# Routing by pairs of heads, dot products that write to PSUM, and a row ring over dead activations, in a one-core decoder block

## The chip, the cores and the metric

The kernel runs on one core of a Trainium2 chip. The metric is device time in microseconds (us) of one launch; lower is better. Engines are named as in the profile: PE (TensorE matmul), PEld (its weight load), DVE (VectorE), ACT (ScalarE), POOL (GpSimd), SP (SyncE, which here only issues DMAs).

## What is computed

One decoder block over 256 tokens of 2048 features, all in float32. The first half (projection, sliding-window attention, retention, gates, output projection) is not touched. The second half is a product-key expert layer:

```python
qry = (xt @ w_query).reshape(T, H, 2, 128)                 # H = 8 heads
s = jnp.einsum('thpd,phnd->thpn', qry, sub_keys)           # 2 x 128 scores a head
top_s, top_i = lax.top_k(s, 16)
cand_s = top_s[:, :, 0, :, None] + top_s[:, :, 1, None, :]
best_s, best_pos = lax.top_k(cand_s.reshape(T, H, 256), 16)
expert_idx = ...                                           # 128 experts a token, of 16384
gates = jax.nn.softmax(best_s, axis=-1)
act = gelu(einsum('td,thkd->thk', xt, expert_down[expert_idx]))
y = einsum('thk,thkd->td', gates * act, expert_up[expert_idx])
out = rmsnorm(h + y, final_norm)
```

## The kernel before, in words

Tokens lie on the 128 partitions in two blocks (`NB = 2`). A matrix product in float32 is done as three passes over operands that are split in a high and a low part: ACT casts a weight unit to `whi` (L107), DVE subtracts to get `wlo` (L108), PE does three matmuls (L138 to L140, L154 to L156). A unit is 4 x 128 rows of 512 columns (1 MB), loaded by SP into a ring of three `raw` tiles; `whi` and `wlo` are rings of three half units. Units are requested two ahead.

The expert layer's stages follow one another:

- **Queries.** Four products of 4 units (`gemm(h_ops, 4)`). After each, `query_scores` makes the scores `sc` for 4 lists of 128 keys (two heads) in each token block.
- **Routing** (DVE): `top16` finds the 16 best of a list with five instructions; `candidates`, `cand_top`, `ranks` and `pick` follow for all 8 heads of a token block; `indices` writes `ix`, the row numbers.
- **gemm1.** The dot products with all 16384 experts over features 0 to 1407, in 32 tiles of 512 experts. A tile is two split units (48 matmuls of 512 columns) and a third unit of 3 x 128 features that PE takes directly as float32 (L161; operand `htf`, the sum of `hth` and `htl`). The result goes to `a_dram`.
- **Dots.** The remaining 640 features: for each of the 256 (block, choice) pairs POOL gathers one expert row of 640 floats per token by an indirect DMA (`fetch_u`, L605), and DVE multiplies it with `hg` and sums (`dot`, L613). The elementwise product goes to `djunk`, which nobody reads.
- **Tail.** For each of the 256 pairs POOL gathers the score from `a_dram` (`score`, L640; 14 ahead) and the 2048-wide row of `expert_up` (`fetch`, L583), in one fixed line; DVE adds weight times row to `ys` in PSUM (L689).

What DVE has to do besides the split is queued by `later(cost, ...)`, and `drain(budget)` takes from that queue after every unit. This settles the order in which code is emitted; a list scheduler with a simulated timeline then sets the order on each engine, and units that are prefetched have priority. Each engine runs its instructions strictly in that order. Rows of both kinds share one ring of `VR = 8` tiles of 2048 floats in the pool `v`, which takes the place of the routing's tiles once routing is over.

Of the kernel before, what the change touches and what calls it, by code (L numbers as in the profile page):

```python
# [16 lines left out]
OP = mybir.AluOpType  # L17
# [12 lines left out]
BG_NATIVE = 4.9  # L30
CF = 8
CN = 3
CG = NC - CF - CN
GC = CG * P
G0 = D - GC
DOT = 0.85
VR = 8
GRP = 8
LEAD = 14


@with_exitstack
def hybrid_block(ctx, tc, x, x_t, anorm, fnorm, frow, w_in, w_ab, w_rb, w_out, w_q, skeys, down, down_n, down_g, up, sinks, fin,
# [26 lines left out]
    for t in range(NT):  # L70
        units += [down[t, u] for u in range(CF // 4)] + [down_n[t]]
# [16 lines left out]
    def emit_unit(u):  # L88
        if units[u].shape[1] == CN:
            nat = stream.tile([P, 4, 512], F32, name="raw", bufs=3)  # L90
            nc.sync.dma_start(nat[:, :CN], units[u])
            ready[u] = nat
            return
        raw = stream.tile([P, 4, 512], F32, name="raw", bufs=3)
        if u == 0:
            for i in range(4):
                nc.sync.dma_start(raw[:, i], units[u][:, i])
        else:
            nc.sync.dma_start(raw, units[u])
        hs = []  # L100
        for i in range(2):
# [3 lines left out]
            for k in range(0, 2, step):  # L105
                src = raw[:, 2 * i + k:2 * i + k + step]
# [37 lines left out]
    def gemm_mixed(ops, xf):  # L144
        ps = [acc.tile([P, 512], F32, name="acc") for _ in range(NB)]
        for u in range(CF // 4):
            hs = next_unit()
            for k in range(4):
                hi, lo = hs[k // 2]
                wh, wl = hi[:, k % 2], lo[:, k % 2]  # L150
                c = u * 4 + k
                for b in range(NB):
                    xh, xl = ops(c, b)
                    nc.tensor.matmul(ps[b], lhsT=xh, rhs=wh, start=(c == 0), stop=False)  # L154
                    nc.tensor.matmul(ps[b], lhsT=xh, rhs=wl, start=False, stop=False)  # L155
                    nc.tensor.matmul(ps[b], lhsT=xl, rhs=wh, start=False, stop=False)  # L156
            drain(BG_RATE)
        nat = next_unit()
        for k in range(CN):
            for b in range(NB):  # L160
                nc.tensor.matmul(ps[b], lhsT=xf[:, k, b * P:(b + 1) * P], rhs=nat[:, k], start=False,  # L161
                                 stop=(k == CN - 1))
        drain(BG_NATIVE)
# [24 lines left out]
    xth = keep.tile([P, NC, T], F32R, name="xth", tag="xh")  # L188
    xtl = keep.tile([P, NC, T], F32R, name="xtl", tag="xl")
# [249 lines left out]
    hth = keep.tile([P, NC, T], F32R, name="hth", tag="xh")  # L439
    htl = keep.tile([P, NC, T], F32R, name="htl", tag="xl")  # L440
# [16 lines left out]
    htf = peer.tile([P, CN, T], F32, name="htf")  # L457
    nc.vector.tensor_add(htf, hth[:, CF:CF + CN].bitcast(F32), htl[:, CF:CF + CN].bitcast(F32))
# [15 lines left out]
    top = rp.tile([P, NB, NC, 16], F32, name="top")  # L474
    topi = rp.tile([P, NB, NC, 16], U32, name="topi")
# [16 lines left out]

    def query_scores(b, j, ps):
# [10 lines left out]
        sc = rp.tile([P, 4, P], F32, name="sc", bufs=6)  # L504
        nc.scalar.copy(sc, pt)
        for i in range(4):
            later(1.0, top16, top[:, b, 4 * j + i], topi[:, b, 4 * j + i], sc[:, i])

    for j in range(4):
        ps = gemm(h_ops, 4)  # L510
        for b in range(NB):
            query_scores(b, j, ps[b])

    rb = [dict() for _ in range(NB)]

    def candidates(b):
        tif = rp.tile([P, NC, 16], BF16, name="tif")
        nc.vector.tensor_copy(tif, topi[:, b])
        cand = rp.tile([P, 8, 136], F32, name="cand")
        tv = top[:, b].rearrange("p (h s) k -> p h s k", s=2)  # L520
        nc.vector.tensor_add(cand[:, :, :128].rearrange("p h (a c) -> p h a c", c=16),
                             tv[:, :, 0, :8, None].to_broadcast([P, 8, 8, 16]),
                             tv[:, :, 1, None, :].to_broadcast([P, 8, 8, 16]))
        nc.vector.tensor_add(cand[:, :, 128:], tv[:, :, 0, 8:], tv[:, :, 1, 0:1].to_broadcast([P, 8, 8]))
        best = rp.tile([P, 8, 16], F32, name="best")
        pos = rp.tile([P, 8, 16], U32, name="pos")
        rb[b].update(tif=tif, cand=cand, best=best, pos=pos)

    def cand_top(b, hd):
        d = rb[b]  # L530
        top16(d["best"][:, hd], d["pos"][:, hd], d["cand"][:, hd])

    def ranks(b):
        d = rb[b]
        bits = rp.tile([P, 2, 8, 16], U32, name="bits")
        nc.vector.tensor_single_scalar(bits[:, 0], d["pos"], 4, op=OP.logical_shift_right)
        nc.vector.tensor_single_scalar(bits[:, 1], d["pos"], 15, op=OP.bitwise_and)
        rf = rp.tile([P, 2, 8, 16], F32, name="rf")
# [7 lines left out]
        ga = rp.tile([P, 8, 16], F32, name="ga")  # L546
        best = d["best"]
        nc.vector.tensor_sub(ga, best, best[:, :, 0:1].to_broadcast([P, 8, 16]))
        nc.scalar.activation(ga, ga, AF.Exp)
        gs = rp.tile([P, 2, 8], F32, name="gs")  # L550
        nc.vector.tensor_reduce(gs[:, 0], ga, axis=AX.X, op=OP.add)
        nc.vector.reciprocal(gs[:, 1], gs[:, 0])
        nc.vector.tensor_mul(sel[:, 2, b].rearrange("p (h k) -> p h k", h=8), ga,
                             gs[:, 1, :, None].to_broadcast([P, 8, 16]))

    def pick(b, s):
        d = rb[b]
# [8 lines left out]
        nc.vector.tensor_add(sel[:, s, b].rearrange("p (h k) -> p h k", h=8), oh[:, :, 0], oh[:, :, 1])  # L566

    for b in range(NB):
        later(2.0, candidates, b)
        for hd in range(8):  # L570
            later(1.0, cand_top, b, hd)
        later(2.0, ranks, b)
        later(4.6, pick, b, 0)
        later(4.6, pick, b, 1)
    ix = peer.tile([P, 2, NB, P], U32, name="ix")
    vtiles = {}
    vp = {}

    def fetch(n):
        v = vp["pool"].tile([P, D], F32, name="v", bufs=VR)  # L580
# [5 lines left out]
    def indices():  # L586
        rt.close()
        msk.close()
        tmp2 = pool("tmp2")
        ef = tmp2.tile([P, 2, NB, P], F32, name="ef")  # L590
        nc.vector.scalar_tensor_tensor(ef[:, 0], sel[:, 0], 128.0, sel[:, 1], op0=OP.mult, op1=OP.add)
        for b in range(NB):
            nc.vector.tensor_scalar_add(ef[:, 1, b], ef[:, 0, b], rows[:, b:b + 1])
        nc.vector.tensor_copy(ix, ef)
        vp["pool"] = pool("v")
        vp["ps"] = pool("ysum", space=PSUM)
        for n in range(VR):
            fetch_u(n)
# [160 lines left out]
```

## Time and profile before

| | |
|---|---|
| median of 3 runs | 2119.17 us (2112.92 to 2120.25) |
| the profiled execution: time, span | 2116.2 us, 2114.4 us |
| PE, DVE, POOL busy | 1387.9, 1556.2, 918.4 us |
| first query matmul | 776.9 us |
| gemm1, first and last matmul | 873.1, 1411.7 us |
| dots, first and last | 971.5, 1397.0 us |
| first score gather, last `expert_up` gather | 1422.2, 2086.7 us |

Times inside the span count from its start. A share of the whole span says little here, since each stage has another limit; the stages are read apart.

### The profile page before, as it was taken

The page shows a single profiled execution, that of the slowest core. Times are in us where ns is not written, and L with a number is a line of the kernel's source. Part 1 is how long each engine was busy: PE and PEld are TensorE (multiplying, and loading weights), DVE is VectorE, ACT ScalarE, POOL GpSimd, SP SyncE. Part 2 cuts the span into 40 slices and gives each one's busy share as a digit, 9 for nine tenths or more (in the row PEclk, how much of TensorE's full clock was granted, in tenths as well). Part 3 has the DMA queues.
Part 4 walks back from the last instruction along what each step waited for, and adds up shares of the span by engine and source line. Part 5 has one row for each costly group of instructions (what it writes and reads, how often), then busy time and mean ns, then how long its engine had stood idle before and what let it go on. Part 6 is the DMA issues. An engine that isn't in the chain of part 4 may idle for free.

```text
span 2114.4 us, 18649 instructions
## 1 busy us (share of the span) xinstructions
PE 1387.9 (66%) x5864; PEld 1076.1 (51%) x5864; DVE 1556.2 (74%) x2037; ACT 614.7 (29%) x780; POOL 918.4 (43%) x802
## 2 busy tenths in 40 slices
PE   8999999999999999999999999960000000000000
PEld 6888888888888888866666676640000000000000
DVE  5676576544544567796777877748989899999998
ACT  6555444444444454433333333310000001000001
POOL 0101001000000000006888888857777777777773
PEclk9999999999999999999999999985555555555555
DMA  8545545655555564559999999987999999999997
GB/s 313 183 151 176 175 144 197 221 197 187 193 189 192 191 231 162 176 194 325 406 406 391 391 408 408 396 353 271 395 397 395 399 399 384 410 400 407 399 400 307
DMA packets 114516, 630.24 MB, mean 298 GB/s; under 512 B 21872, under 2 KB 22512, under 8 KB 54000
## 3 DMA queue, kind: packets, MB, share of 16 engines
q0 software_dynamic: 65536, 352.50, 42.3%
q1 hardware_dynamic: 38016, 253.77, 33.0%
q10 hardware_dynamic: 10864, 22.77, 2.8%
q8 instruction: 46, 0.75, 0.1%
q14 instruction: 54, 0.44, 0.1%
HBM read 610.10 MB, written 18.87 MB: 297 GB/s over the span
## 4 chain that ended last, share of the span: by engine, by line
PE 47%; DMA 20%; issue 17%; POOL 8%; DVE 8%; POOLq 0%; ACT 0%; ACTq 0%; DVEq 0%; SPq 0%
PE acc L139 13%; PE acc L138 13%; PE acc L140 13%; DMA v<-in_down_g_dram,ix 11%; DMA v<-in_up_dram,ix 6%; DVE ys L689 4%; POOL v L583 4%; POOL wsel L640 3%; PE acc L161 2%; DMA wsel<-a_dram,ix 2%; DVE wlo L108 1%; PE acc L155 1%; PE acc L156 1%; PE acc L154 1%; POOL v L605 1%
## 5 line engine op out<-in xcount | busy, mean ns | idle before, releaser
L108 DVE TENSOR_TENSOR wlo<-raw,whi 128x1024 fp32r<-128x1024 f32 (+1 forms) x426 | 526.1, 1236 | 332.9 <-ACT whi L107 332.5
L107 ACT CAST whi<-raw 128x1024 fp32r<-128x1024 f32 (+1 forms) x426 | 443.8, 1048 | 667.7 <-PE acc L140 367.5
L689 DVE SCALAR_TENSOR_TENSOR ys<-v,wsel,ys 128x2048 f32<-128x2048 f32 x254 | 598.3, 2355 | 30.8 <-DMA v<-in_up_dram,ix 23.3
L605 POOL DMA_INDIRECT v<-in_down_g_dram,ix x256 | 347.5, 1357 | 353.0 <-ACT whi L107 273.0
L640 POOL DMA_INDIRECT wsel<-a_dram,ix x256 | 259.1, 1012 | 96.4 <-issue 93.0
L583 POOL DMA_INDIRECT v<-in_up_dram,ix x256 | 260.9, 1019 | 80.7 <-issue 58.7
L613 DVE SCALAR_TENSOR_TENSOR djunk<-v,rs_r,hg 128x640 bf16<-128x640 f32 x256 | 219.2, 880 | 99.6 <-DMA v<-in_down_g_dram,ix 99.0
L139 PE MATMUL acc<-wlo,xth 128*128 128x512 f32 x736 | 291.9, 397 | 0.0
L140 PE MATMUL acc<-whi,xtl 128*128 128x512 f32 x736 | 288.2, 392 | 0.0
L138 PE MATMUL acc<-whi,xth 128*128 128x512 f32 x736 | 266.7, 394 | 9.1 <-ACT whi L107 9.1
L155 PE MATMUL acc<-wlo,hth 128*128 128x512 f32 x512 | 203.8, 398 | 13.1 <-DVE wlo L108 12.9
L156 PE MATMUL acc<-whi,htl 128*128 128x512 f32 x512 | 200.1, 391 | 0.0
L154 PE MATMUL acc<-whi,hth 128*128 128x512 f32 x512 | 191.4, 411 | 2.2 <-ACT whi L107 2.2
L681 ACT ACTIVATE wsel<-wsel 128x8 f32<-128x8 f32 x32 | 6.6, 208 | 595.9 <-DVE wsel L680 533.7
L161 PE MATMUL acc<-raw,htf 128*128 128x512 f32 x384 | 169.9, 592 | 0.0
L138 PEld LDWEIGHTS acc<-whi,xth 128*128 128x128 f32 x736 | 138.7, 189 | 38.3 <-ACT whi L107 9.5
L139 PEld LDWEIGHTS acc<-wlo,xth 128*128 128x128 f32 x736 | 138.8, 189 | 29.7 <-DVE wlo L108 1.0
L140 PEld LDWEIGHTS acc<-whi,xtl 128*128 128x128 f32 x736 | 138.8, 189 | 28.1 <-issue 0.2
L433 POOL TENSOR_TENSOR sg<-sg 128x512 f32<-128x512 f32 x8 | 14.1, 1790 | 291.8 <-DVE sg L432 291.8
L155 PEld LDWEIGHTS acc<-wlo,hth 128*128 128x128 f32 x512 | 96.1, 188 | 42.9 <-DVE wlo L108 22.2
L154 PEld LDWEIGHTS acc<-whi,hth 128*128 128x128 f32 x512 | 96.1, 188 | 33.5 <-issue 12.2
L161 PEld LDWEIGHTS acc<-raw,htf 128*128 128x128 f32 x384 | 72.7, 189 | 79.1 <-issue 76.6
(185 smaller groups left out, 1483.7 us busy)
## 6 DMA issues: line engine op xcount, KB each, us to landing
raw<-in_w_in_dram SPq DMA_DIRECT2D x91, 1024.0 KB, 4.8
raw<-in_down_dram SPq DMA_DIRECT2D x64, 1024.0 KB, 8.9
raw<-in_down_n_dram SPq DMA_DIRECT2D x32, 768.0 KB, 6.7
raw<-in_w_rb_dram SPq DMA_DIRECT2D x16, 1024.0 KB, 4.8
raw<-in_w_out_dram SPq DMA_DIRECT2D x16, 1024.0 KB, 4.8
raw<-in_w_q_dram SPq DMA_DIRECT2D x16, 1024.0 KB, 4.8
a_dram<-a ACTq DMA_DIRECT2D x32, 512.0 KB, 12.2
raw<-in_w_ab_dram SPq DMA_DIRECT2D x8, 1024.0 KB, 4.9
```

Source lines behind the costliest of these rows:

```text
L107: nc.scalar.copy(hi[:, k:k + step], src)
L108: nc.vector.tensor_sub(lo[:, k:k + step], src, hi[:, k:k + step].bitcast(F32))
L138: nc.tensor.matmul(ps[b], lhsT=xh, rhs=wh, start=(c == 0), stop=False)
L139: nc.tensor.matmul(ps[b], lhsT=xh, rhs=wl, start=False, stop=False)
L140: nc.tensor.matmul(ps[b], lhsT=xl, rhs=wh, start=False, stop=(c == last))
L154: nc.tensor.matmul(ps[b], lhsT=xh, rhs=wh, start=(c == 0), stop=False)
L155: nc.tensor.matmul(ps[b], lhsT=xh, rhs=wl, start=False, stop=False)
L161: nc.tensor.matmul(ps[b], lhsT=xf[:, k, b * P:(b + 1) * P], rhs=nat[:, k], start=False, stop=(k == CN - 1))
L583: return nc.gpsimd.indirect_dma_start(v, None, up, IndirectOffsetOnAxis(ap=ix[:, 0, b, k:k + 1], axis=0), bounds_check=NE - 1)
L605: nc.gpsimd.indirect_dma_start(u[:, :GC], None, down_g, IndirectOffsetOnAxis(ap=ix[:, 0, b, k:k + 1], axis=0), bounds_check=NE - 1)
L640: return nc.gpsimd.indirect_dma_start(wsel[:, b, k:k + 1], None, a_flat, IndirectOffsetOnAxis(ap=ix[:, 1, b, k:k + 1], axis=0), bounds_che ...
L689: nc.vector.scalar_tensor_tensor(ys, v, w[:, kk:kk + 1], ys, op0=OP.mult, op1=OP.add)
```

## The change

- Routing goes by query tile: after each of the four query products the two heads of that tile, in both token blocks (`G4 = 4` groups), are routed to the end, `indices` included. After the first of these, 9 rows are fetched.
- The rows of the dots get a ring of their own (`UR = 9` tiles of 640 floats); the dots go in the order of the head pairs; their elementwise output goes to `ys`, a PSUM tile that is free until the tail.
- `hth` and `htl` are kept as two halves each. The 2048-wide rows have 5 tiles of their own, and 4 that lie over these halves: two are dead after the queries, two after gemm1. The first 7 of these rows are asked for by the last dots.
- Tile 0 of gemm1 is taken wholly as float32 (`ALL_NATIVE = 1`: 22 products instead of 48 split matmuls and 6), so `htf` has 11 chunks and is made by POOL. In the 16 query units POOL does the second half's subtraction.
- The costs and budgets of the DVE queue are new (`DOT` 0.85 to 1.06, `top16` 1.0 to 1.4).

```diff
+CD = 11
+ALL_NATIVE = 1
-DOT = 0.85
-VR = 8
+DOT = 1.06
+UR = 9
+VR = 5
...
-            step = 1 if u == 0 else 2
+            m = min(2, n - i)
+            step = 1 if u == 0 else m
...
-                nc.vector.tensor_sub(lo[:, k:k + step], src, hi[:, k:k + step].bitcast(F32))
+                eng = nc.gpsimd if i and base - 16 <= u < base else nc.vector
+                eng.tensor_sub(lo[:, k:k + step], src, hi[:, k:k + step].bitcast(F32))
...
+                    if u in native:
+                        nc.tensor.matmul(ps[b], lhsT=xf[:, c, b * P:(b + 1) * P], rhs=w[:, k], start=first, stop=last)
+                        continue
...
-    htf = peer.tile([P, CN, T], F32, name="htf")
-    nc.vector.tensor_add(htf, hth[:, CF:CF + CN].bitcast(F32), htl[:, CF:CF + CN].bitcast(F32))
+    htf = peer.tile([P, CD, T], F32, name="htf")
+    for c in range(0, CD, 4):
+        e = min(c + 4, CD)
+        nc.gpsimd.tensor_add(htf[:, c:e], hth[:, c:e].bitcast(F32), htl[:, c:e].bitcast(F32))
...
     def fetch(n):
-        v = vp["pool"].tile([P, D], F32, name="v", bufs=VR)
+        r = n % (VR + 4)
+        if r < VR:
+            v = vp["pool"].tile([P, D], F32, name="v", bufs=VR)
+        else:
+            v = vp["more"][r - VR]
...
+    def fetch_u(m):
+        u = peer.tile([P, GC], F32, name="u", bufs=UR)
+        b, k = seq[m]
...
+    def dot(m):
+        u = utiles.pop(m)
+        b, k = seq[m]
+        nc.vector.scalar_tensor_tensor(vp["junk"][:, :GC], u, rstd2[:, b:b + 1], hg[:, b], op0=OP.mult, op1=OP.mult,
+                                       accum_out=sdot[:, b, k:k + 1])
+        if m + UR < NB * P:
+            fetch_u(m + UR)
+        elif m + UR - NB * P < VR + 2:
+            fetch(m + UR - NB * P)
+
+    for j in range(4):
+        ps = gemm(h_ops, 4)
+        later(0.0, open_heads, j)
+        for b in range(NB):
+            with tc.high_priority(50000):
+                sc = query_scores(b, j, ps[b])
+            for i in range(4):
+                later(1.4, head_top, j, b, i, sc[:, i])
+        later(1.3, candidates, j)
+        for g in range(G4):
+            later(1.4, cand_top, j, g)
+        later(1.0, ranks, j)
+        later(2.7, pick, j, 0)
+        later(2.7, pick, j, 1)
+        later(0.7, indices, j)
+        later(0.8, gates, j)
```

What stands on POOL's queue behind the gates' products (L433, L455 in the new file) was this before (L605 the dots' rows, L583 the `expert_up` rows, L640 the scores):

```order
L433 TENSOR_TENSOR sg<-sg 128x512 x8
L605 DMA v<-in_down_g_dram,ix 128x640 x256
L583 DMA v<-in_up_dram,ix 128x2048 x8
L640 DMA wsel<-a_dram,ix 128x1 x15
L583 DMA v<-in_up_dram,ix 128x2048
```

and is now this (L130 the subtraction, L482 `htf`, L638 the dots' rows, L630 the `expert_up` rows, of which `mxh` and `mxl` are those over the halves, L698 the scores):

```order
L130 TENSOR_TENSOR wlo<-raw,whi 128x1024 x11
L638 DMA u<-in_down_g_dram,ix 128x640 x2
L130 TENSOR_TENSOR wlo<-raw,whi 128x1024
L638 DMA u<-in_down_g_dram,ix 128x640 x7
L130 TENSOR_TENSOR wlo<-raw,whi 128x1024 x3
L630 DMA mxh_7284<-in_up_dram,ix 128x2048
L630 DMA mxl_7285<-in_up_dram,ix 128x2048
L638 DMA u<-in_down_g_dram,ix 128x640 x28
L630 DMA v<-in_up_dram,ix 128x2048 x5
L638 DMA u<-in_down_g_dram,ix 128x640 x219
L698 DMA wsel<-a_dram,ix 128x1 x14
L630 DMA mxh_10672<-in_up_dram,ix 128x2048
```

Ahead of these stand one more subtraction and the three pieces of `htf`. Nine row fetches now stand between the query stage's subtractions, and seven `expert_up` rows stand ahead of most of the dots' rows instead of behind them.

On DVE, the last of gemm1's subtractions and dots before the tail's first instructions were, before (a tile has four L108):

```order
L613 SCALAR_TENSOR_TENSOR djunk,sdot<-v,rs_r,hg 128x640 x4
L108 TENSOR_TENSOR wlo<-raw,whi 128x1024
L613 SCALAR_TENSOR_TENSOR djunk,sdot<-v,rs_r,hg 128x640
L108 TENSOR_TENSOR wlo<-raw,whi 128x1024
L613 SCALAR_TENSOR_TENSOR djunk,sdot<-v,rs_r,hg 128x640 x3
L108 TENSOR_TENSOR wlo<-raw,whi 128x1024 x2
L680 TENSOR_TENSOR wsel<-wsel,sdot 128x8
```

and are now:

```order
L645 SCALAR_TENSOR_TENSOR ys,sdot<-u,rs_r,hg 128x640 x7
L130 TENSOR_TENSOR wlo<-raw,whi 128x1024
L645 SCALAR_TENSOR_TENSOR ys,sdot<-u,rs_r,hg 128x640
L130 TENSOR_TENSOR wlo<-raw,whi 128x1024
L645 SCALAR_TENSOR_TENSOR ys,sdot<-u,rs_r,hg 128x640 x2
L130 TENSOR_TENSOR wlo<-raw,whi 128x1024
L645 SCALAR_TENSOR_TENSOR ys,sdot<-u,rs_r,hg 128x640
L130 TENSOR_TENSOR wlo<-raw,whi 128x1024
L645 SCALAR_TENSOR_TENSOR ys,sdot<-u,rs_r,hg 128x640 x7
L130 TENSOR_TENSOR wlo<-raw,whi 128x1024 x24
L740 TENSOR_TENSOR wsel<-wsel,sdot 128x8
```

A tile's four subtractions stood with 10 dots in the steady part and stand with 11 now (7 + 1 + 2 + 1); 2 subtractions followed the last dot, and 24 follow it now. The first dot stood behind the subtractions of about five tiles and all routing; now it stands behind four subtractions (tile 1's), in the midst of the last head pair's routing, and 33 dots stand ahead of the last subtraction of tile 5.

## Rows read from the trace of the kernel before

**Rows 1.** Stretches of the span: busy us (instructions) by engine, granted clock, DMA.

```profile
core 0: us, PE busy (x) PEld busy (x) DVE busy (x) ACT busy (x) POOL busy (x), PEclk, DMA share, GB/s
850.00:900.00 50.00, 50.00 (x235) 40.05 (x234) 39.40 (x165) 21.98 (x27) 0.00 (x0) 1.00 0.49 168
900.00:950.00 50.00, 47.78 (x177) 32.82 (x176) 48.01 (x158) 17.50 (x21) 0.00 (x0) 1.00 0.62 205
963.00:1398.00 435.00, 421.94 (x1553) 289.99 (x1552) 331.62 (x615) 141.06 (x156) 353.33 (x261) 1.00 1.01 397
1400.00:1410.00 10.00, 10.00 (x40) 7.11 (x39) 1.22 (x1) 0.09 (x1) 2.92 (x3) 1.00 1.02 421
1600.00:1700.00 100.00, 0.00 (x0) 0.00 (x0) 91.26 (x47) 0.83 (x4) 76.58 (x76) 0.50 1.00 395
```

**Rows 2.** Timeline of PE in gemm1: start us, busy us; the 12 float32 matmuls of a tile.

```profile
1208.05 5.31 PE L161 MATMUL acc<-raw,htf 128*128 128x512 f32 x12
1224.13 5.31 PE L161 MATMUL acc<-raw,htf 128*128 128x512 f32 x12
```

**Rows 3.** The dots' row fetches: ns min/median/max, first and last start; idle us before, times.

```profile
L605 POOL DMA_INDIRECT v<-in_down_g_dram,ix x256: 1007/1307/2168, 963.2 to 1389.6; - x128
...
  issue: 39.3, 129
  DVE wlo L108: 16.2, 53
...
DMA to landing us min/median/max: 4.7/8.3/11.2
```

**Rows 4.** Waits from 960 to 1412 us: us in total, times, longest.

```profile
DVE djunk L613 <- DMA v<-in_down_g_dram,ix: 99.0, 82, 4.5
...
PEld acc L155 <- DVE wlo L108: 22.0, 23, 3.5
```

**Rows 5.** Timeline of DVE and POOL among the dots: start us, duration us.

```profile
1101.41 0.88 DVE L613 SCALAR_TENSOR_TENSOR djunk<-v,rs_r,hg 128x640 bf16<-128x640 f32 x1
1101.54 1.64 POOL L605 DMA_INDIRECT v<-in_down_g_dram,ix  x1 [0.30 <-DVE wlo L108]
...
1118.64 1.01 POOL L605 DMA_INDIRECT v<-in_down_g_dram,ix  x1 [0.30 <-issue]
```

**Rows 6.** Timeline in the tail: DVE's adds into `ys`, POOL's gathers, the last gather.

```profile
1503.49 9.53 DVE L689 SCALAR_TENSOR_TENSOR ys<-v,wsel,ys 128x2048 f32<-128x2048 f32 x4
1504.19 1.01 POOL L640 DMA_INDIRECT wsel<-a_dram,ix  x1 [0.30 <-issue]
1505.50 1.01 POOL L583 DMA_INDIRECT v<-in_up_dram,ix  x1 [0.30 <-issue]
...
2086.73 1.01 POOL L583 DMA_INDIRECT v<-in_up_dram,ix  x1 [0.30 <-issue]
```

**Rows 7.** Timeline at gemm1's end: last subtraction, last eviction, first score gather.

```profile
1400.12 1.22 DVE L108 TENSOR_TENSOR wlo<-raw,whi 128x1024 fp32r<-128x1024 f32 x1 [0.37 <-ACT whi L107]
...
1412.34 0.69 ACT L467 ACTIVATE a<-acc,rs_r 128x512 f32<-128x512 f32 x1 [0.17 <-PE acc L161]
...
1422.22 1.02 POOL L640 DMA_INDIRECT wsel<-a_dram,ix  x1 [18.69 <-issue]
```

**Rows 8.** Timeline of DVE in the query stage: four lists of the routing.

```profile
811.24 0.87 DVE L487 MAX8 top<-sc 128x8 f32<-128x128 f32 x4 [0.56 <-ACT sc L505]
812.03 0.07 DVE L488 MATCH_VALUE_LOAD topi<-top,sc 128x8 f32 x1
...
813.08 0.07 DVE L489 MATCH_VALUE_LOAD sc<-top,sc 128x8 f32 x1
```

**Rows 9.** POOL's elementwise instructions of the gates, one line: durations as in rows 3.

```profile
L433 POOL TENSOR_TENSOR sg<-sg x8: 1291/1790/2292, 455.3 to 687.9; 128x512 f32<-128x512 f32 x8
```

**Rows 10.** Timeline of POOL and DVE in the gates' stage.

```profile
455.32 3.54 POOL L433 TENSOR_TENSOR sg<-sg 128x512 f32<-128x512 f32 x2 [71.09 <-DVE sg L432]
456.13 1.56 DVE L108 TENSOR_TENSOR wlo<-raw,whi 128x1024 fp32r<-128x1024 f32 x1 [0.30 <-ACT whi L107]
```

More of the change, by code (lines that the diff above doesn't have):

```diff
@@ L29, with __init__, __getitem__ @@
 BG_RATE = 2.8
[L30 to L33, printed above, removed]
+NATIVE_RATE = 1.65
+CD = 11
+CG = NC - CD
+ALL_NATIVE = 1
 GC = CG * P
 G0 = D - GC
-DOT = 0.85
-VR = 8
+DOT = 1.06
+UR = 9
+VR = 5
 GRP = 8
 LEAD = 14
+class Halves:
+    def __init__(self, pool, name, tag):
+        self.parts = [pool.tile([P, NC // 2, T], F32R, name=f"{name}{i}", tag=f"{tag}{i}") for i in range(2)]
+    def __getitem__(self, key):
+        c = key[1]
+        i = (c.start if isinstance(c, slice) else c) // (NC // 2)
+        if isinstance(c, slice):
+            c = slice(c.start - 8 * i, c.stop - 8 * i)
+        else:
+            c -= 8 * i
+        return self.parts[i][(key[0], c) + tuple(key[2:])]
 @with_exitstack
@@ L503, in query_scores @@
             nc.tensor.matmul(pt[:, i], lhsT=qt[:, i], rhs=sk[:, 4 * j + i], start=True, stop=True)
-        sc = rp.tile([P, 4, P], F32, name="sc", bufs=6)
+        sc = rp.tile([P, 4, P], F32, name="sc", bufs=8)
         nc.scalar.copy(sc, pt)
[L506 to L514, printed above, removed]
@@ L587, in indices, with routed @@
+    def routed():
         rt.close()
         msk.close()
[L589 to L594, printed above, removed]
         vp["pool"] = pool("v")
         vp["ps"] = pool("ysum", space=PSUM)
-        for n in range(VR):
-            fetch_u(n)
@@ L620, in hybrid_block @@
-    later(4.0, indices)
-    for n in range(NB * P):
-        later(DOT, dot, n)
-    rows = cst.tile([P, NB], F32, name="rows")
-    nc.scalar.dma_start(rows, rows_d)
-    fbc = peer.tile([P, D], F32, name="fbc")
-    nc.scalar.dma_start(fbc, bass.AP(tensor=fin.tensor, offset=fin.offset, ap=[[0, P], [1, D]]))
+        vp["junk"] = vp["ps"].tile([P, D], F32, name="ys")
+        fbc = vp["pool"].tile([P, D], F32, name="fbc")
+        nc.scalar.dma_start(fbc, bass.AP(tensor=fin.tensor, offset=fin.offset, ap=[[0, P], [1, D]]))
@@ L629, in hybrid_block @@
+        vp["fbc"] = fbc
+        vp["more"] = [keep.tile([P, D], F32, name=f"m{t}1", tag=f"{t}1") for t in ("xh", "xl")]
+    later(0.0, routed)
+    for m in range(NB * P):
+        later(DOT, dot, m)
     for t in range(NT):
@@ L631, in hybrid_block @@
     drain(1e9)
+    vp["more"] += [keep.tile([P, D], F32, name=f"m{t}0", tag=f"{t}0") for t in ("xh", "xl")]
     wsel = peer.tile([P, NB, P], F32, name="wsel")
@@ L654, in hybrid_block @@
         in_line(score, n)
+    for n in range(VR + 2, VR + 4):
+        in_line(fetch, n)
     def finish(b, ys):
```

199 lines of the change are left out of this document (104 added, 95 removed).

## The prediction

> **What bounds the kernel now.** I read the stretches of the span first, since the share of the whole span mixes stages. In the query stage PE is busy for all 50 of 50 us; just behind it, in routing, DVE is, with 48.0 of 50, and PE loses 2.2 [rows 1]. In the stretch of the dots PE is busy for 421.9 of 435 us, DVE for 331.6, POOL for 353.3, and the DMA engines' share is 1.01 at 397 GB/s [rows 1]. So the next view is the one of POOL's row fetches there. Before all fetches but the first POOL idles only the same 0.30 us (53 times in 16.2 us, 129 in 39.3), whatever ended it [rows 3]: it never waits for a free tile or a landing. The pitch is (1389.6 - 963.2) / 255 = 1.67 us a row [rows 3], while DVE waits 99.0 us for rows and PE's weight loads wait 22.0 us for `wlo` [rows 4], which DVE delivers late because it stands at a dot whose row has not landed. A tile of gemm1 takes PE 16.08 us where it isn't held up [rows 2]; ten dots go with a tile, 16.7 us. So the row stream sets gemm1's pace, PE is a close second, and the last score can't be gathered before the last tile is evicted and written: last eviction at 1412.3, first score at 1422.2 [rows 7]. From there POOL paces the tail: a score and a row every 2 x 1.31 = 2.62 us, against 9.53 / 4 = 2.38 of DVE [rows 6].
>
> Why is the pitch 1.67? The timeline shows it. A fetch takes 1.01 us while DVE is idle, and 1.64 when it starts 0.13 us after a dot [rows 5]: the dot runs to 1102.22 by the start of its accumulator read, 0.68 us into the fetch, and 0.63 is what the fetch is longer. In the tail, where DVE is busy nearly always with an instruction that has one operand in SBUF and the other and the result in PSUM, a gather takes 1.01 us throughout [rows 6]. The stretch, 0.35 us a fetch at the median and the mean, is thus DVE's SBUF work.
>
> **Query stage: POOL's subtractions.** No row has a subtraction of 1024 columns on POOL. Nearest are the gates' products: 1.29 us for 512 columns alone, 2.29 at most beside DVE [rows 9]; twice that is 2.6 to 4.6 us. I take 3.1, since DVE works there for about 0.8 of the time [rows 1] but most of routing's instructions are 0.2 us long [rows 8]. 16 of them are 50 us, `htf` (22 x 128 columns for its two blocks) 7 to 12.6, nine fetches 9 x 1.31 to 1.67 = 12 to 15: 69 to 101 us of POOL, in the 97 us between first query and first gemm1 matmul. On average it fits; locally it doesn't. Two fetches stand ahead of one subtraction and seven ahead of the next three, so these are 2 and 5 to 7 us late, where DVE delivered a subtraction of 1.22. PE has no slack there, so I take 5 us (bounds 0 and 10).
>
> The block works the other way too: DVE's subtraction beside a gate's product took 1.56 instead of 1.22 us [rows 10]. Sixteen times 0.3 to 1 us is 5 to 16 us of DVE. Routing of three head pairs must be over before tile 1's first subtraction. A list of 128 costs 0.79 / 4 + 1.05 / 4 = 0.46 us for its first two passes, about 1.18 for five [rows 8]; an estimate from such prices for three pairs (8 lists and 4 merged lists each, 12 x 1.2, and 9 for the rest, 23 us a pair, one pair after the other from the scores of the first query tile, near 808, with first-half subtractions of 1.22 between) is that the third pair is done near 891, and 5 to 16 later with the blocks. Cover for this is the float32 tile 0: 44 matmuls of (5.31 - 0.2) / 12 = 0.43 us [rows 2], 18.9 us, needs no subtraction. So routing itself costs nothing beyond the 5 us; without the cover it would be 10 to 15 more.
>
> **Tile 1's start.** 873.1 + 18.9 + 2 (last scores) + 5, and 2 for DVE's part: 901, where tile 1 started at 889 before (873.1 + 16.08). The float32 tile is 2.8 us longer on PE, and saves DVE 4 x 1.22.
>
> **The rows.** 33 dots, not none, stand ahead of tile 5's last subtraction, and 37 rows can be fetched before the last head pair is routed. But then POOL stands: five `expert_up` rows come next, and their pool takes the place of the routing's tiles, so it opens when the last `indices` is done, behind 18 subtractions, tile 5's second, and 28 dots. That is 901 + 62 = 963, the moment at which the first fetch goes now. Eight microseconds for the five (5 x 1.67), then 219 rows: the last is issued at 971 + 218 x pitch and lands 8.3 us later [rows 3].
>
> What is the pitch? Lower bound 1.31, a fetch never stretched [rows 6]; upper 1.67, as now, or slightly more as DVE has 11 dots with a tile. The dot still reads two operands in SBUF, as the subtraction does, and only its result moves; the tail's unblocked instruction has one. The trace has no instruction with two SBUF operands and a PSUM result, so what the edit does is not shown. The nearer case by operands is the blocked one, and subtractions block in any case. I take 1.65. Sum: 971 + 360 + 8 = 1339 for the last dot.
>
> The Trainium skill, page "SBUF — State Buffer", section "SBUF: two separate sides", says that VectorE and GpSimd lock a shared port pair for a whole instruction, and that VectorE takes it in a 2-port mode or with two SBUF inputs, the latter only against a GpSimd instruction that reads SBUF. By this rule the dot blocks as before, and the time is the sum below; if instead the SBUF output was the cause, it is the first rival. The tail's 1.01 us agrees with the rule; a gather's index list lies in SBUF.
>
> **gemm1's end.** Behind the last dot stand 24 subtractions, six tiles, where 2 stood. Until then tiles go at 11 x 1.65 = 18.2 us; then rows no longer hold anything, and PE needs 6 x 16.08 = 96.5 us with POOL idle. From last dot to last eviction, with 1 to 2 us for the first of these: 1437, 25 later than 1412.3. What is saved by dots that begin early is lost, as the work that could have covered them stands alone at the end.
>
> **Tail.** The write that the first score waits for lands sooner beside an idle DMA: of the 9.9 us from eviction to score [rows 7] I take off 2. The first seven rows already lie in SBUF before as now eight; the line of scores and fetches has the same pitch, 2.62, so 2086.7 - 1422.2 stays [rows 6]. Sum against the profiled execution: 2116.2 + 25 - 2 = 2139 us. That execution is 3 us under the median; half a per cent, about 10.6 us, is what a measurement of this kernel can tell from no change.
>
> **Rivals.**
> *The PSUM result does unblock POOL.* Then DMA paces: from 963 to the last dot go 5 x 1.05 + 219 x 0.328 MB of rows and the weights and scores of 21 tiles (3.41 MB each, sizes from shapes), 150 MB with a 1 MB load. At 404 to 421 GB/s (421 is the highest that a row shows [rows 1]) that is 355 to 371 us: last dot at 1321 to 1333, end 6 to 18 us before the sum, 2121 to 2133. For it: POOL's only stretch is DVE's. Against: the operands.
> *Faster: the row stream keeps up with PE.* A pitch of 16.08 / 11 = 1.46 us or less lets PE set the pace: 894 + 31 x 16.08 = 1392.5, 20 before now, with the tail 2094; with the 7 us of late start 2101. It decides below a pitch of about 1.49 us and needs 11 rows and 3.41 MB in 16.08 us, 436 GB/s. Against: that exceeds the 421; for: 1.31 is POOL's own limit, and DVE needs 4 x 1.22 + 11 x 0.88 = 14.6 us a tile.
> *POOL starves PE in the queries.* With subtractions at 4.6 us, 16 are 73 and the whole is 101 us against 97, each late by more than the last; tile 1 begins 10 to 20 us later still, and the end does: 2147 to 2158. For: 2.29 [rows 9]. Against: routing's short instructions.
> That the change doesn't do what it says is the main case already, in which the PSUM result frees nothing.
>
> **How the numbers follow.** Main case 0.5, 2128 to 2150 (pitch 1.60 to 1.68, slip 0 to 15); unblocked POOL 0.2; PE's pace 0.15; starved queries 0.15. Faster by over 0.5% (under 2108) is PE's pace, 0.14. Within (to 2129.8): three quarters of the unblocked case and a little of the main one, 0.2. Slower: 0.66. The range from 2104 to 2154 leaves out most of PE's pace and the starved case's upper part, 0.1 each.
>
> **What would show it.** Right: fetches of the dots stretched beside a dot by what is left of it, pitch 1.6 to 1.68; a POOL stop until about 963; last dot near 1339, then six tiles at 16.08 us with the DMA share far below 1; first score near 1445 and 692 us from there to the end. Wrong: a constant 1.01 us beside dots (first rival), tiles of 16.1 us among the dots (second), POOL's subtractions above 4 us with PE waiting for `wlo` in the queries (third). A start of tile 1 far from 901, or dots that DVE, not the rows, holds back, would upset the sum itself.

## The result, and the profile after

2179.28 us median (2178.62 to 2183.83), against 2119.17 before: 1.0298 times, 95% interval 1.0285 to 1.0312. It is slower, as forecast, but by 60 us where 20 were forecast, and outside the stated range. The profiled execution took 2183.83 us, span 2182.0.

The stretches of the span of the changed kernel, columns as in [rows 1]; its gemm1 ends 70 us later, so a stretch behind its last dot (1385 us) is added:

```profile
850.00:900.00 50.00, 43.38 (x165) 31.02 (x164) 49.97 (x228) 12.40 (x17) 22.11 (x15) 0.93 0.55 185
900.00:950.00 50.00, 50.00 (x196) 34.60 (x195) 46.74 (x166) 18.57 (x23) 13.06 (x12) 1.00 0.84 293
963.00:1398.00 435.00, 383.74 (x1351) 262.07 (x1350) 320.06 (x573) 118.98 (x135) 319.19 (x233) 0.95 0.97 367
1386.00:1484.00 98.00, 96.88 (x360) 67.63 (x360) 29.30 (x26) 32.06 (x35) 0.00 (x0) 1.00 0.58 187
1600.00:1700.00 100.00, 0.00 (x0) 0.00 (x0) 91.46 (x50) 1.04 (x5) 76.69 (x77) 0.50 1.01 400
```

In the same 435 us of dots PE is busy for 383.7 us instead of 421.9. Behind the last dot it works for 98 us with POOL idle and the DMA share at 0.58. The tail is as it was. So the loss lies before the first score, and the lines that POOL's gathers have in the source view (columns as in [rows 3]) date it: last row fetch at 1373.9 instead of 1389.6, first score at 1488.5 instead of 1422.2 [rows 7].

```profile
L638 POOL DMA_INDIRECT u<-in_down_g_dram,ix x256: 1006/1474/2054, 856.5 to 1373.9; - x128
...
  DVE ys L645: 37.0, 101
...
  DVE wlo L130: 15.6, 40
  DMA v<-in_up_dram,ix: 12.8, 4
```

```profile
L698 POOL DMA_INDIRECT wsel<-a_dram,ix x256: 1004/1015/1461, 1488.5 to 2144.8; - x128
```

POOL now stands before its row fetches, 12.8 us in four times until a row of `expert_up` lands. The timeline of POOL shows where:

```profile
977.85 1.63 POOL L630 DMA_INDIRECT v<-in_up_dram,ix  x1 [0.30 <-ACT a L491]
...
985.00 1.00 POOL L630 DMA_INDIRECT v<-in_up_dram,ix  x1 [0.30 <-issue]
986.31 1.02 POOL L638 DMA_INDIRECT u<-in_down_g_dram,ix  x1 [0.30 <-issue]
...
993.66 1.74 POOL L638 DMA_INDIRECT u<-in_down_g_dram,ix  x1 [3.69 <-DVE wlo L130]
996.89 1.01 POOL L638 DMA_INDIRECT u<-in_down_g_dram,ix  x1 [1.50 <-DMA v<-in_up_dram,ix]
1003.37 1.01 POOL L638 DMA_INDIRECT u<-in_down_g_dram,ix  x1 [5.47 <-DMA v<-in_up_dram,ix]
1008.70 1.01 POOL L638 DMA_INDIRECT u<-in_down_g_dram,ix  x1 [4.32 <-DMA v<-in_up_dram,ix]
1011.22 1.01 POOL L638 DMA_INDIRECT u<-in_down_g_dram,ix  x1 [1.51 <-DMA v<-in_up_dram,ix]
```

The five `expert_up` rows went out from 977.9 to 986.0, and the dots' rows behind them didn't land for long. The timeline of DVE and the stretches show what stood still meanwhile: a dot waited 16.86 us for its row, PE did nothing from 1000 to 1010, and the DMA engines were full.

```profile
1011.37 0.90 DVE L645 SCALAR_TENSOR_TENSOR ys<-u,rs_r,hg 128x640 f32<-128x640 f32 x1 [16.86 <-DMA u<-in_down_g_dram,ix]
...
1018.22 0.89 DVE L645 SCALAR_TENSOR_TENSOR ys<-u,rs_r,hg 128x640 f32<-128x640 f32 x1
...
1019.20 0.89 DVE L645 SCALAR_TENSOR_TENSOR ys<-u,rs_r,hg 128x640 f32<-128x640 f32 x1
```

```profile
1000.00:1005.00 5.00, 0.00 (x0) 0.00 (x0) 0.00 (x0) 0.00 (x0) 1.01 (x1) 0.61 1.02 424
1005.00:1010.00 5.00, 0.00 (x0) 0.00 (x0) 0.00 (x0) 1.04 (x1) 1.01 (x1) 0.50 1.02 413
```

PE stood from 999.2 to 1014.4, for the subtraction that DVE does behind that dot; the line is in the next fence. The last two lines of the DVE fence show a second thing: dots that follow each other start 0.98 us apart, not 0.80. Third, PE's timeline: in the queries it waits for a subtraction of POOL, whose own timeline has seven row fetches just ahead of it. Tile 1 begins at 909.8, and its float32 part stands at 921.7.

```profile
874.27 0.50 PE L161 MATMUL acc<-wlo,hth 128*128 128x512 f32 x1 [3.25 <-POOL wlo L130]
...
909.77 0.70 PE L181 MATMUL acc<-whi,hth 128*128 128x512 f32 x2
...
921.69 5.31 PE L177 MATMUL acc<-raw,htf 128*128 128x512 f32 x12
...
1014.44 0.79 PE L182 MATMUL acc<-wlo,hth 128*128 128x512 f32 x1 [15.27 <-DVE wlo L130]
...
1478.82 5.31 PE L177 MATMUL acc<-raw,htf 128*128 128x512 f32 x12
```

```profile
870.84 1.01 POOL L638 DMA_INDIRECT u<-in_down_g_dram,ix  x1 [0.30 <-issue]
871.86 4.68 POOL L130 TENSOR_TENSOR wlo<-raw,whi 128x1024 fp32r<-128x1024 f32 x2
```

### The profile page after: what moved, and what is told of

The parts are those of the page before. It is cut to its first block, busy times and chain, and to the rows that moved or that the text cites. A ratio compares the mean times of both kernels' runs of the same rounds, so it can differ in the third digit from the quotient of the medians.

```text
span 2182.0 us, 18689 instructions
## 1 busy us (share of the span) xinstructions
PE 1413.8 (65%) x5848; PEld 1087.1 (50%) x5848; DVE 1579.3 (72%) x2086; ACT 606.7 (28%) x778; POOL 963.8 (44%) x821
## 4 chain that ended last, share of the span: by engine, by line
PE 52%; DMA 16%; DVE 16%; issue 10%; POOL 5%; ACT 1%; POOLq 0%; ACTq 0%; DVEq 0%; SPq 0%
PE acc L161 11%; PE acc L162 11%; PE acc L160 11%; DVE ys L749 10%; PE acc L177 6%; DMA u<-in_down_g_dram,ix 5%; DMA v<-in_up_dram,ix 4%; DMA wsel<-a_dram,ix 4%; PE acc L182 4%; PE acc L183 4%; PE acc L181 3%; DVE wlo L130 2%; DMA mxl<-in_up_dram,ix 2%; POOL wsel L698 1%; POOL v L630 1%
## 5 line engine op out<-in xcount | busy, mean ns | idle before, releaser
L130 DVE TENSOR_TENSOR wlo<-raw,whi 128x1024 fp32r<-128x1024 f32 (+1 forms) x406 | 506.0, 1248 | 404.4 <-ACT whi L128 404.1
L128 ACT CAST whi<-raw 128x1024 fp32r<-128x1024 f32 (+1 forms) x422 | 438.0, 1047 | 578.5 <-PE acc L162 369.4
L638 POOL DMA_INDIRECT u<-in_down_g_dram,ix x256 | 346.5, 1354 | 145.5 <-DVE ys L645 37.0
L698 POOL DMA_INDIRECT wsel<-a_dram,ix x256 | 259.9, 1015 | 190.7 <-DMA a_dram<-a 113.0
L749 DVE SCALAR_TENSOR_TENSOR ys<-v,wsel,ys 128x2048 f32<-128x2048 f32 x142 | 334.6, 2356 | 5.0
L645 DVE SCALAR_TENSOR_TENSOR ys<-u,rs_r,hg 128x640 f32<-128x640 f32 x256 | 228.8, 894 | 73.8 <-DMA u<-in_down_g_dram,ix 69.8
L177 PE MATMUL acc<-raw,htf 128*128 128x512 f32 x416 | 184.0, 592 | 0.0
L630 POOL DMA_INDIRECT v<-in_up_dram,ix x144 | 146.3, 1016 | 43.9 <-issue 32.0
L455 POOL TENSOR_TENSOR sg<-sg 128x512 f32<-128x512 f32 x8 | 14.1, 1787 | 291.8 <-DVE sg L454 291.8
L749 DVE SCALAR_TENSOR_TENSOR ys<-mxh,wsel,ys 128x2048 f32<-128x2048 f32 x56 | 131.9, 2356 | 2.5 <-DMA mxh<-in_up_dram,ix 0.7
L749 DVE SCALAR_TENSOR_TENSOR ys<-mxl,wsel,ys 128x2048 f32<-128x2048 f32 x56 | 131.9, 2356 | 2.0
## 6 DMA issues: line engine op xcount, KB each, us to landing
a_dram<-a ACTq DMA_DIRECT2D x32, 512.0 KB, 10.4
```

Source lines behind the costliest of these rows:

```text
L130: eng.tensor_sub(lo[:, k:k + step], src, hi[:, k:k + step].bitcast(F32))
L177: nc.tensor.matmul(ps[b], lhsT=xf[:, c, b * P:(b + 1) * P], rhs=w[:, k], start=first, stop=last)
L638: nc.gpsimd.indirect_dma_start(u, None, down_g, IndirectOffsetOnAxis(ap=ix[:, 0, b, k:k + 1], axis=0), bounds_check=NE - 1)
L698: return nc.gpsimd.indirect_dma_start(wsel[:, b, k:k + 1], None, a_flat, IndirectOffsetOnAxis(ap=ix[:, 1, b, k:k + 1], axis=0), bounds_che ...
L749: nc.vector.scalar_tensor_tensor(ys, v, w[:, kk:kk + 1], ys, op0=OP.mult, op1=OP.add)
```

## The experiments

The runs were made in five groups, each with the kernel before measured on the same chip. In two groups (e1 to e4; e14 to e17) that kernel takes 2116 us, in the other three 2155 to 2159. The difference lies in the tail: from the first score to the end the changed kernel takes 693.5 us in the one case and 735.5 in the other (e13), with 377 GB/s from 1600 to 1700 us and not 400. Up to the first score the two agree within 4 us (1488.5 and 1484.4 us for the changed kernel). So the ratios and the moment of the first score are compared, not the microseconds of runs of different groups, and 4 us at the first score decide nothing.

**Single parts of the changed kernel.** The dots' results back in SBUF, in one tile:

```diff
-        nc.vector.scalar_tensor_tensor(vp["junk"][:, :GC], u, ...
+        junk = peer.tile([P, GC], BF16, name="djunk", bufs=1)
+        nc.vector.scalar_tensor_tensor(junk, u, ...
```

> The changed kernel, but the dots' elementwise result goes to a bf16 tile in SBUF again. The schedule then places 12 instead of 11 dots with a tile at first and leaves 28 instead of 24 subtractions behind the last dot, so the last dot, not the end, is to be read. Theory A (the PSUM result makes a dot that follows a dot 0.18 us longer, and the row fetches, which start only when a dot has ended, fall into step with that): dot to dot 0.81 instead of 0.99 us, median fetch 1.3 instead of 1.47 us, rows from 1012 us on every 1.65 instead of 1.72 us, last dot about 15 us before 1385, time 2165 to 2180 with the one tile more that is left behind. Theory B (the rows are paced by the DMA engines or by the number of dots with a tile, not by where the result goes): fetch and pitch as in the changed kernel, last dot within 4 us of 1385, time 2180 to 2200.

Measured: 2174.21 us, 1.0283 (1.0253 to 1.0313). Last dot at 1359.8, median fetch 1.42 us, first score at 1478.5; the one tile let dots follow at 0.93 us, not 0.81, and the wait behind the `expert_up` rows was still there (18.3 us). The last dot came 25 us earlier, more than the edit can have given by itself, as the order had changed with it; one tile more behind it took most of that back. It doesn't separate the theories: of A's signs the time came, the 0.81 us and the fetch of 1.3 didn't.

The `expert_up` rows behind the last row of the dots:

```diff
+            with tc.issue_after(vp["last_u"].ins):
                 fetch(m + UR - NB * P)
```

> The changed kernel, but all seven early rows of expert_up are queued on POOL behind the last row of the dots instead of ahead of 219 (two of them of 247). Theory A (the five rows of 1 MB each stand in the way of the dots' rows for about 17 us: POOL's row fetches wait for tiles from 989 to 1011 us and DVE for 16.9 us): that wait is gone, last dot 15 to 19 us earlier than 1385, time 2160 to 2166. Theory B (that wait comes from something else, such as the ring of nine tiles or the end of routing): a wait of over 10 us stays near 1000 us, time 2172 to 2182.

Measured: 2159.06 us, 1.0208 (1.0179 to 1.0237), last dot at 1362.3, first score at 1466.6. Theory A, and a little more than it said: the last dot comes 23 us earlier and not 15 to 19, the first score 22 us (18 against e13), and the longest wait of a dot is gone. The order of dots and subtractions within the tiles changed with the edit, still with 11 dots to a tile; but 20 us are there already at the 46th row, the first behind the stop (992.6 instead of 1012.5). From the view of waits, 960 to 1412 us (total, times, longest):

```profile
DVE ys L646 <- DMA u<-in_down_g_dram,ix: 81.4, 69, 3.5
```

The kernel before with its dots' results in PSUM, and the changed kernel with two parts of the PSUM tile by turns:

```diff
+        if "junk" not in vp:
+            vp["junk"] = vp["ps"].tile([P, D], F32, name="ys")
-        nc.vector.scalar_tensor_tensor(junk, u[:, :GC], ...
+        nc.vector.scalar_tensor_tensor(vp["junk"][:, :GC], u[:, :GC], ...
...
+        o = 1024 * (m % 2)
+        nc.vector.scalar_tensor_tensor(vp["junk"][:, o:o + GC], u, ...
```

> The kernel before, with the one edit that the dots' elementwise result goes to a PSUM tile; the order of the instructions stays. Theory A (PSUM result is slower and POOL goes in step with it): dot to dot 0.99 instead of 0.81 us, row pitch 1.72 to 1.82 instead of 1.67 us, time 2132 to 2157. Theory B (where the result goes is hidden, since DVE waits 99 us for rows anyway): 2114 to 2124.

> The changed kernel, with the dots' elementwise results going by turns to two parts of the PSUM tile that share no bank. Theory A1 (a dot waits until the same place in PSUM has been written): dot to dot 0.81 us, last dot about 15 us earlier, time 2160 to 2168. Theory A2 (each dot with a PSUM result takes that long to give its sum back, wherever it writes): dot to dot stays 0.99 us, time 2176 to 2184.

Measured: 2125.28 us, 1.0039 (1.0022 to 1.0055), and 2177.89 us, 1.0294 (1.0268 to 1.0321). In the kernel before, whose order stays the same, the result's place costs about 8 us by the ratio, between the ranges of the two theories: there is a cost, but less than A's. In the profiled execution, the slowest of ten, the first score comes at 1433.7 instead of 1422.2, and the last 210 rows go at 1.72 instead of 1.67 us. Two parts change nothing (A2): 0.99 us from dot to dot stay.

`hg` in PSUM too, so that a dot has one operand in SBUF:

```diff
+            nc.scalar.copy(vp["junk"][:, GC * (1 + b):GC * (2 + b)], hg[:, b])
...
+        hp = vp["junk"][:, GC * (1 + b):GC * (2 + b)]
-        nc.vector.scalar_tensor_tensor(vp["junk"][:, :GC], u, rstd2[:, b:b + 1], hg[:, b], ...
+        nc.vector.scalar_tensor_tensor(vp["junk"][:, :GC], u, rstd2[:, b:b + 1], hp, ...
```

> The changed kernel, with the second factor of the dots, hg, copied to PSUM once, so that a dot reads one operand in SBUF and one in PSUM and writes PSUM, as the tail's adds do. Theory A (a row fetch on POOL is held up by a DVE instruction with two operands in SBUF): fetches take 1.01 us beside a dot and are stretched by subtractions alone, median 1.01 to 1.1 instead of 1.47 us, pitch under 1.60; then the rows come as fast as the DMA engines can, last dot 20 to 40 us before 1385, time 2135 to 2165. Theory B (any DVE instruction that touches SBUF holds it up, or the tail's gathers are unhindered for another reason): median stays above 1.3 us, time 2170 to 2190.

Measured: 1.0156 (1.0139 to 1.0173), last dot at 1353.5, first score at 1453.9, 31 to 35 us earlier than in the two profiles of the changed kernel; the last 210 rows go at 1.58 us. Theory A. The order within the tiles changed here too, as in e2, but the fetches show the effect by themselves: in the source view's line the median takes 1.015 us, and on the timeline a fetch that starts 0.31 us after a dot has begun isn't stretched.

```profile
L638 POOL DMA_INDIRECT u<-in_down_g_dram,ix x256: 1009/1015/2070, 854.9 to 1341.5; - x128
```

```profile
1102.99 0.89 DVE L646 SCALAR_TENSOR_TENSOR ys<-u,rs_r,ys 128x640 f32<-128x640 f32 x1
1103.30 1.01 POOL L638 DMA_INDIRECT u<-in_down_g_dram,ix  x1 [0.30 <-DVE ys L646]
```

The queries' subtractions on DVE again:

```diff
-                eng = nc.gpsimd if i and base - 16 <= u < base else nc.vector
+                eng = nc.vector
```

> The changed kernel, with the 16 subtractions of the query stage on DVE again. Theory A (PE loses about 10 us at the end of the query stage because POOL's 2.4 us subtractions stand behind row fetches): PE no longer waits for wlo in the queries, but DVE has 16 x 1.14 = 18 us more to do before the third head pair is routed; tile 1's float32 part starts 0 to 10 us later than 921.7, time 2175 to 2192. Theory B (the subtractions on POOL cost more than they free): tile 1 starts 5 to 9 us earlier, time 2168 to 2175.

Measured: 1.021 (1.0193 to 1.0227), tile 1's float32 part at 908.6, first score at 1468.8. Theory B, and more than it said: 13 us earlier at tile 1, 16 to 20 at the first score (against the same two profiles). PE is busy for all of 830 to 880 us there.

**All of it, and the spread of the dots.** The next kernels have the first rows asked for behind POOL's last subtraction, the `expert_up` rows last, and the dots put by hand: `PER` of them to a tile from tile `FIRST`, each behind the newest subtraction.

```diff
+    def pace(t, part):
+        if t < FIRST:
+            return
+        state["due"] += PER * part
+        while dots and state["due"] >= 1.0 and ...:
+            with tc.issue_after(state["sub"].ins):
+                dot(dots.popleft())
+            state["due"] -= 1.0
```

> The changed kernel with four edits: dots' results in SBUF, rows of expert_up behind all rows of the dots, the first rows asked for behind the last subtraction of POOL, and the dots spread by hand, 8 or 9 behind each tile's subtractions from tile 1 to the last. Theory A (the loss is mostly the dots packed 11 to a tile, so that rows hold up PE there, and six tiles without rows behind them): rows no longer hold up PE, tiles of 16.1 us from tile 1 to the end, last eviction near 1405 to 1412, time 2105 to 2122. Theory B (early routing itself or the DMA engines cost the time): last eviction stays above 1430, time above 2135.

> The same as e8_even_sbuf in order and edits, but the dots' results stay in PSUM. Theory A: where rows and DVE have slack, 0.18 us more a dot is mostly covered: within 8 us of e8_even_sbuf, and 2105 to 2128. Theory B (the PSUM result holds up the row fetches by itself): 15 us or more slower than e8_even_sbuf.

Measured: e8 (8.6 to a tile) 0.9943 (0.9926 to 0.9959), first score 1410.8; e10 0.9952 (0.9935 to 0.9969), 1412.1. Theory A in both: about half a per cent faster than the kernel before, and the place of the result doesn't count where rows have slack. Then the changed kernel once more, and two of its parts undone without the even spread:

> The changed kernel, unedited, on the chip of the three runs beside it. Its ratio to the kernel before is the measure for them. Every theory: 1.026 to 1.031 times the kernel before.

> The changed kernel with results in SBUF and the rows of expert_up behind the dots' rows, but the dots where the scheduler puts them, 26 subtractions behind the last. Theory A (what the packed dots and the bare tiles behind them cost is a term of its own, about 40 us): the two edits together bring the last dot to 1335 to 1345, the first score to 1447 to 1460, time 1.012 to 1.020 times the kernel before. Theory B (the two edits are the whole loss): 1.00 or below.

Measured: 1.0284 (1.0266 to 1.0301), and 1.0191 (1.017 to 1.0211) with the last dot at 1341 and the first score at 1464 (A, but for the first score, which it had at 1460 at most). So the two edits are not the whole loss, and how the dots are packed may be the rest. That was tested alone, with e8's edits and 10 or 11 dots to a tile, 24 subtractions behind the last dot:

```diff
-PER = 8.6
+PER = 10.6
```

> As e8_even_sbuf in every edit, but the dots go 11 to a tile, as in the changed kernel, so that 24 subtractions follow the last one. Theory A (packing costs by itself: rows at 1.65 us hold a tile of 11 at 18.2 us, and six tiles stand bare): tiles of 17 to 18.5 us among the dots, last dot 1335 to 1350, first score 1440 to 1455, 1.005 to 1.017 times the kernel before (e8_even_sbuf 0.994). Theory B (the even spread gained because of another of its edits): below 1.000.

> As e14_packed_sbuf in order and edits, but the dots' results go to PSUM. Theory A (where dots are packed and rows are short, 0.18 us more from dot to dot lengthens the row pitch, as POOL starts a fetch when a dot ends): pitch 0.05 to 0.09 us longer than in e14_packed_sbuf, last dot and first score 10 to 20 us later, 0.005 to 0.010 more in the ratio. Theory B (PSUM costs nothing even there): within 0.002 of e14_packed_sbuf.

> As e14_packed_sbuf, but two SBUF tiles by turns take the dots' results, as in the kernel before; e14's single one left 0.93 us from dot to dot, not 0.81. The steady part of the order is the same. Theory A (the time from dot to dot counts where rows are short, and e14 hid it by having most of the loss too): dot to dot 0.81 us, row pitch 0.03 us or more shorter, 1.005 to 1.013 times the kernel before. Theory B (rows and fetches set the pace of packed tiles whatever a dot takes): 1.014 to 1.020, as e14 and e15.

Measured: e14 1.0177 (1.0157 to 1.0198), last dot 1347.5, first score 1457.9; e15 1.0191 (1.017 to 1.0212), 1349.0 and 1459.7; e18 1.0126 (1.0109 to 1.0143), 1336.6 and 1448.6. Packing costs 0.0234 of the time before, about 50 us (e14 against e8; A, just beyond its slow end). e15 against e14 is B, but e14's single tile had dots at 0.93 us, so this tests 0.06 us from dot to dot and no more. With two tiles, 0.81, the first score comes 11 us before e15's and the ratio is as A says. That this is the time from dot to dot is not shown: against its expectation, e18's dots stand otherwise among the subtractions than e14's up to tile 20, and 7 of the 11 us are there already at the 46th row; the last 210 rows go at 1.655 us, where e15's go at 1.673 and e14's at 1.679: 4 us, and less than A's 0.03 a row. The stretch 1030 to 1330 us, in e14 and then in e8 (columns as in [rows 1]):

```profile
1030.00:1330.00 300.00, 276.38 (x984) 187.82 (x985) 230.01 (x423) 86.78 (x96) 242.16 (x179) 0.98 0.99 382
```

```profile
1030.00:1330.00 300.00, 299.87 (x1118) 209.81 (x1117) 229.47 (x395) 103.72 (x114) 224.69 (x161) 1.00 1.00 387
```

With 179 rows in 300 us, 1.68 us each, PE does 276 us of work; with 161 rows it does 299.9. The DMA engines move about the same in both, since e8 has more weights beside fewer rows.

**Towards a faster kernel.** All five take e8, with the queries' subtractions on DVE again and the first rows asked for behind the newest of them. e11 and e12 have 9.4 dots to a tile from tile 4, e12 with tile 0 split (`ALL_NATIVE = 0`); e16 and e19 have 8.9 from tile 2, e19 with two SBUF tiles for the results; e17 has `hg` and results in PSUM and 9.1 from tile 3. The edit of e12 against e11, and those of e19 against e8:

```diff
-ALL_NATIVE = 1
+ALL_NATIVE = 0
```

```diff
-FIRST = 1
-PER = 8.6
+FIRST = 2
+PER = 8.9
...
-                eng = nc.gpsimd if i and base - 16 <= u < base else nc.vector
+                eng = nc.vector
...
-                with tc.issue_after(state["psub"].ins):
+                with tc.issue_after(state["sub"].ins):
...
-        junk = peer.tile([P, GC], BF16, name="djunk", bufs=1)
+        junk = peer.tile([P, GC], BF16, name="djunk", bufs=2)
```

> As e8_even_sbuf, but DVE does all subtractions of the query stage, and the dots go 9 or 10 to a tile from tile 4 on. Theory A (POOL's subtractions and row fetches delay tile 1 by some 10 us and the rest of the kernel with it): float32 part of tile 1 at 909 instead of 916 us, tiles of 16.1 us behind it, first score near 1403, 0.989 to 0.993 times the kernel before. Theory B (DVE, with 18 us more to do, or the later dots hold up PE later on): first score above 1411, 0.995 or more.

> As e11_even_dve_subs, and tile 0 goes as two split units and one float32 unit, as in the kernel before. Theory A (routing fits beside gemm1's tiles as it did before, so the float32 tile costs its 2.8 us and gives nothing back once the dots begin at tile 4): first score 2 to 8 us before that of e11_even_dve_subs, 0.985 to 0.991 times the kernel before. Theory B (the float32 tile covers DVE's routing): tiles 1 to 4 wait for wlo, first score later than in e11_even_dve_subs.

> As e8_even_sbuf, but DVE does the subtractions of the queries, and the dots go 9 to a tile from tile 2. Theory A (e11 and e12 lost on rows that came too late and 9.4 to a tile, not on DVE's subtractions): tile 1 near 909 as in e11, tiles nearly all 16.1 us, first score 1404 to 1412, 0.988 to 0.994 times the kernel before. Theory B (DVE's work there holds routing up so long that rows are short later): 0.997 or more.

> As e16_dve_subs_early, but hg and the dots' results lie in PSUM, so a dot has one operand in SBUF, and the dots go 9 to a tile from tile 3. Theory A (then only subtractions hold row fetches up, and rows are never short although they begin late): median fetch 1.01 to 1.1 us, all tiles 16.1 us from tile 1 on, first score 1398 to 1406, 0.986 to 0.992 times the kernel before. Theory B (DVE itself, or the DMA engines, run short): 0.996 or more.

> As e16_dve_subs_early, with two SBUF tiles by turns for the dots' results. Theory A: DVE has about 0.1 us less from dot to dot, but nothing waits for it in evenly spread tiles: within 0.002 of e16 (0.992). Theory B (it counts there too): 0.988 or less.

Measured: e11 1.0019 (1.0009 to 1.003), e12 1.0004 (0.9993 to 1.0015), first scores 1425.7 and 1422.6: theory B for e11, as the dots began at 950 and their rows held PE up again; of e12 the 3 us against e11 came, the ratio didn't. e16 0.9921 (0.9904 to 0.9937; 2099.33 us beside 2115.76), first score 1404.0: A. e17 0.9947 (0.9931 to 0.9964): rows are never short (0.2 us of waiting in all), but the first score, 1406.9, comes no earlier, as PE is the bound already; the ratio missed. e19 0.99 (0.9883 to 0.9916): first score 1403.8, as A says, and the lowest ratio, though its interval overlaps with e16's. Its last tile, and the first score, on the timeline:

```profile
1392.48 5.31 PE L179 MATMUL acc<-raw,htf 128*128 128x512 f32 x12
...
1403.82 1.02 POOL L717 DMA_INDIRECT wsel<-a_dram,ix  x1 [19.55 <-issue]
```

## Why the prediction was wrong

The chain was right: rows set the pace of the dots, six tiles without rows follow, and the tail is as before. The terms behind the last dot came out: the six tiles took 1386 to 1484, the first score came 4.3 us behind the last eviction where 8 were assumed, and from there to the end it took 693.5 us (692.2 before). The last dot was forecast at 1339 and started at 1385. The 46 us divide over three terms ahead of it, of about the same size.

- **"Eight microseconds for the five (5 x 1.67), then 219 rows"** is the step that failed in its mechanism. Issuing them did take 8 us (977.9 to 986.3). But they are 5.2 MB in front of 0.33 MB rows, and the term priced POOL's time and not the transfer: the five landed 15 to 25 us after their issue, and the dots' rows behind them later still. POOL stood too, 15 us beyond the usual gaps, 13 net of fetches that took 1.01 us there. It didn't stand for tiles, as e2's expectation has it: the tiles of these five fetches had been free for 14 to 25 us. Seven gathers were on their way ahead of each of them, and each started 0.77 us after the eighth before it had landed. A weight unit came late as well (ACT waited 10.4 us for it, until 1007.5), but DVE's dot stood longer, until 1011.4. Moving the rows back (e2) brought the 46th row 20 us and the first score 18 to 22 us forward, about the 8 of issuing and the 13 together.
- **"Tile 1's start ... 901"** was 909.8. POOL's subtractions took 2.40 us at the median, less than the 3.1 taken and below the lower bound of 2.6, so their length was not it, and the condition of the rival of starved queries (4.6 us) did not hold. Its effect came in part all the same. That two subtractions stood behind seven fetches was seen, but "I take 5 us (bounds 0 and 10)" was too little, even with the 2 us for DVE's part: in the query stage PE waited 6.9 us for POOL's subtractions and 3.5 for DVE's, where it waited for none before. In e8, whose first rows stand behind POOL's last subtraction, 1.3 of the 6.9 are left (and 5.1 behind DVE's). With all subtractions on DVE tile 1 started 13 us earlier (e7), and DVE managed. The other 5 us of the 9 were not separated; the granted clock was 0.83 from 860 to 880. The last `indices` came with the late start, at 974.8 instead of 963: the first of the 219 rows went at 986.3, not 971.
- **"I take 1.65"**: from 1012.5 to 1373.9 the last 211 rows went at 1.72 (1.70 in e13). The main case held, PSUM results don't free POOL, and rival one fell (its own sum, 963 + 355, starts at 1318 and not at 1321; nothing hangs on it). But 1.65 is less than the 1.67 of the kernel before, which makes 5 of the 15 us. And the text asked only whether the result's place unblocks POOL, and not what it does to DVE: 0.98 instead of 0.80 us from dot to dot. In the kernel before that step alone made the rows 0.05 us slower (e3), which over 210 rows would be the other 10. That it does as much in the packed tiles of the changed kernel is not shown: e15, e14 and e18 don't isolate it. The last row landed 3 us later than taken.

So 15 (start) + 13 (transfer) + 15 (pitch) + 3 (landing) = 46: the rest of the chain followed. Of these the transfer is shown by e2 and the wait for POOL's subtractions by e7 and e8; the pitch is argued in part. That what early dots save "is lost, as the work that could have covered them stands alone at the end" was shown by e14 against e8, 50 us, the largest single piece of the difference to a good version; it was in the sum already. The rival in which PE sets the pace was not reached by the change, but e8, e16 and e19 reach it, by fewer rows to a tile and not by a shorter pitch.

e5 agrees with the rule on two SBUF inputs in the Trainium skill, "SBUF — State Buffer", section "SBUF: two separate sides": beside a dot with one operand in SBUF fetches pass at 1.01 us. By that rule a result in PSUM alone doesn't free POOL, and the median fetch of the changed kernel, 1.47 us, agrees.

## What to carry to other kernels

Price a moved gather by its bytes on the queue as well as by its issue: what stands behind it in the same queue waits for the transfer, and so may the engine that issues. When a stream of rows paces a stage, give each tile as many rows as arrive in the tile's own time, over all tiles; packing more saves nothing and leaves bare work at the end. When a result moves to another memory, look at the time from one instruction to the next, not only at its duration, which changed by 0.01 us here.

## What the runs showed of the hardware

- A gather's issue on POOL is held up by a DVE instruction with two SBUF operands, wherever its result goes: median 1.31 us (two SBUF tiles for results), 1.47 (PSUM), and 1.015 with one operand in PSUM.
- With eight gathers on their way POOL started no other: five times around 1000 us the next one started 0.77 us after the oldest had landed, and in the traces of both kernels no gather starts with more than seven others under way. What sets this number was not tested.
- From dot to dot, with a sum given back: 0.81 us with two SBUF tiles by turns, 0.93 with one, 0.99 in PSUM, there with one place or two. Whether the tile or the memory makes the last step was not separated.
- With PE idle from 999.2 us on, its granted clock was at 0.50, the lower level (1.2 GHz), from 1005 to 1015 and full again from 1020. It fell again behind later pauses, to 0.68 from 1100 to 1110, where PE was busy for 6.0 of 10 us. Over 963 to 1398 the mean was 0.95, where it was 1.00 before. What that alone cost was not separated, so a part of PE's loss among the dots may be the clock's.
